# A ring of weight slots moved to multiples of 4 KB in the on-chip memory

## The chip, the core and the metric

The kernel runs on one core of a Trainium2 chip. A core has a matrix engine (TensorE, PE in the profile), a vector engine (VectorE, DVE), a scalar engine (ScalarE, ACT), a general engine (GpSimd, POOL), a sync engine (SyncE, SP) that here issues DMAs, and 16 DMA engines that move data between the chip's HBM and the on-chip memory, the SBUF. The SBUF has 128 partitions; a tile takes the same range of bytes in each of them, and "address" below means the place of that range in a partition. The metric is the device time of one execution in microseconds (us).

## The reference

One decoder layer over 512 tokens of width 1024, all in float32:

```python
h = rmsnorm(x, attn_norm_w[l])
z = h @ w_in[l]
o_a = hgrn2_mixer(...)             # gated linear recurrence, 8 heads
o_b = mla_mixer(...)               # causal attention with low-rank q and kv, 8 heads
y = sigmoid(gate_a) * (o_a @ w_branch_hgrn[l]) + sigmoid(gate_b) * (o_b @ w_branch_mla[l])
x = x + y @ w_out[l]
h = rmsnorm(x, ffn_norm_w[l])
x = x + hierarchical_moe(h, ...)   # 64 experts, each token goes to 2 of one group of 8
return rmsnorm(x, final_norm_w)
```

Every expert is `(silu(xb @ w1) * (xb @ w3)) @ w2`, with w1 and w3 of 1024 x 512 and w2 of 512 x 1024. The three weights of 64 experts are 402.7 MB, and the kernel reads all of them.

## The kernel before, in words

The program has two halves. The first computes the two mixers, the branch products and the output product. Its weights come in pieces of 512 B a row and are split into a high and a low part (L90 and L91), and each product is made of three matrix multiplications (`mm3`). The second half is the experts: 16 blocks of four experts each. A block gathers its tokens by a matrix product (L1069), multiplies by w1 and w3 (`h` in the rows), by w2 (`y`), and adds the rows back to the residual `x2` through another product (`cb` and L1154), for which GpSimd makes a selection matrix out of `slb` (L1088 to L1092).

The experts' weights come as chunks of 8 KB in each partition (1 MB in all). A block has 24 of them. They go through a ring of 22 slots:

```python
RING = ("n",) * 2 + ("y",) + ("x",) * 11 + ("y0",) * 2 + ("wa",) * 2 + ("y2",) * 2 + ("wb",) * 2
```

Each name is a pool of SBUF memory. The slots of `x` (11) lie on the right side of the SBUF, the other 11 on the left side. Where two neighbours are one pool's, they are one tile of 16 KB and one DMA of 2 MB fills both, so that every one of its 128 rows is a single run of 16 KB in HBM and in the SBUF. `prefetch` (L833) issues the DMAs on SyncE's queue in the ring's order. A DMA is issued when the slot's last readers on PE are done. A slot is thus refilled about every 54 us, 27 us for the left slots and 27 us for the right ones. The four w2 parts of the last block come in smaller strips (L845).

Tiles are laid out as they are allocated: pools of the left side grow from address 0 upwards, pools of the right side from the far end downwards, each tile rounded up to 32 B. What stands before the ring on either side sets the addresses of its slots. On the left that is the constants, the small tiles of the pool `keep` (with `rb`, the routers' biases, and `slb`, the slot numbers by block), `small`, and `gl` (with `gT`, the norms' gains). On the right it is `x2` and the experts' working tiles (`xT`, `hid`, `t1`, `owT`, `o1`). In the program as built, every left slot starts 128 B past a multiple of 4096, every right slot 992 B past one; the SBUF is full to its end at 229,344 B.

Of the kernel before, what the change touches and what calls it, by code (L numbers as in the profile page):

```python
# [10 lines left out]
F32 = mybir.dt.float32  # L11
# [9 lines left out]
T = S // 128  # L21
# [11 lines left out]
NB = NE // 4  # L33
# [43 lines left out]
class Trunk:  # L77
# [48 lines left out]
    def run(self):  # L126
        tc, nc, a = self.tc, self.nc, self.a
        const = self.ctx.enter_context(tc.tile_pool(name="const", bufs=1, reuse_waits="tile"))
        cst = const.tile([128, 384], F32, name="cst")
        self.cst = cst  # L130
        self.ident, self.ones, self.iota = [cst[:, i * 128:(i + 1) * 128] for i in range(3)]
        self.keep = self.ctx.enter_context(tc.tile_pool(name="keep", bufs=1, reuse_waits="tile"))
        self.sm = self.ctx.enter_context(tc.tile_pool(name="small", bufs=4, reuse_waits="tile"))
        gl = self.ctx.enter_context(tc.tile_pool(name="gl", bufs=1, reuse_waits="tile"))
        self.ring_open()
        with ExitStack() as right, ExitStack() as left:
            self.mixers(gl, right, left)
        self.moe()


    def mixers(self, gl, right, left):
        tc, nc, a, ident = self.tc, self.nc, self.a, self.ident
        w_in = a["w_in"][0]
        rp = lambda name, bufs=1: right.enter_context(tc.tile_pool(name=name, bufs=bufs, side="right",
                                                                                   reuse_waits="tile"))
# [1 line left out]
        hT = [hp.tile([128, KT, S], F32R, name=f"hT{i}") for i in "hl"]  # L147
        sm = self.sm

        self.gT = gT = gl.tile([128, 46], F32, name="gT")  # L150
        self.fgT = gT[:, 30:38]
        self.lb = gl.tile([128, H], F32, name="lb")
        self.oml = gl.tile([128, H], F32, name="oml")
# [18 lines left out]
        left.close()  # L172


        rc = self.keep
        rb = self.rb = rc.tile([128, 72], F32, name="rb")
        nc.scalar.dma_start(out=rb[:, 0:8], in_=a["router_group_b"].to_broadcast([128, 8]))
        nc.scalar.dma_start(out=rb[:, 8:72], in_=a["router_expert_b"].to_broadcast([128, 64]))
        self.h2p = self.ctx.enter_context(tc.tile_pool(name="h2", bufs=4, reuse_waits="tile"))
# [705 lines left out]
    def route_open(self, rps, gps):  # L885
        nc, mp, iota = self.nc, self.keep, self.iota
        self.rps, self.gps = rps, gps
        self.slb = mp.tile([128, T, 2, NB], F32, name="slb")
        self.wts = mp.tile([128, T, 2], F32, name="wts")
        self.e32 = mp.tile([128, T, 2], F32, name="e32")  # L890
        self.pos = mp.tile([128, T, 2], F32, name="pos")
        self.cnt = mp.tile([128, 1], F32, name="cnt")
        self.fss = mp.tile([128, T], F32, name="fss")
        self.ssq = mp.tile([128, T, 8], F32, name="ssq")
        self.ready = None
        self.h2 = []
        hold = lambda name, shape: mp.tile([128] + shape, F32, name=name)
        self.top = hold("top", [2, T, 8])
        self.ef, self.sl = hold("ef", [T, 2]), hold("sl", [T, 2])
        self.iota8 = hold("iota8", [8])  # L900
        self.fgr = hold("fgr", [8])
        nc.scalar.dma_start(out=self.fgr, in_=self.a["ffn_norm_w"][0].rearrange("(p k) -> p k", k=KT))
        nc.vector.tensor_scalar(out=self.iota8, in0=iota[:, 0:8], scalar1=8.0, scalar2=None, op0=OP.mult)
        self.lps = rps.tile([128, T, 72], F32, name="lgps")
        wr = self.wr
        for kt in range(KT):
            nc.vector.tensor_scalar(out=wr[:, kt], in0=wr[:, kt], scalar1=self.fgT[:, kt:kt + 1],
                                    scalar2=None, op0=OP.mult)
# [382 lines left out]
```

## Time and profile before

| | |
|---|---|
| median of 3 runs | 1597.21 us (1596.31 to 1598.02) |
| the profiled execution's own time | 1594.92 us |
| its span, first to last instruction | 1593.1 us |
| busy share of the span: PE, DVE, ACT, POOL | 86%, 37%, 22%, 15% |
| granted TensorE clock, mean | 0.947 |
| moved by DMA | 458.44 MB, mean 288 GB/s |

PE is busy 86% of the span, but that share is a mean over two halves. The page's lines of 40 slices (a slice is 39.8 us) show the halves: up to slice 17 the DMA engines are busy one to three tenths in most slices, from then on nine tenths. The page's list of the chain of work that ended last goes back from the last instruction through whatever released each step. DMA durations in that chain run from the DMA's issue to its landing, so they hold the time that it stood in the queue.

### The profile page before, as it was taken

The numbers are of one execution on the slowest core, as the hardware profiler recorded it, in microseconds if no ns is written. First come the engines' busy times: TensorE is split into PE (matmuls) and PEld (weight loads), VectorE is DVE, ScalarE is ACT, GpSimd is POOL, SyncE is SP. The second block draws the span as 40 slices with busy tenths as digits, with TensorE's granted clock in tenths as the row PEclk, the third lists the DMA queues.
The fourth block names the chain that finished last, engine by engine and source line by source line (L and its number), as shares of the span: only waits on it lengthen the run. The fifth ranks groups of instructions, "written<-read, shape, count | busy, mean of one in ns | idle before, by whom it ended". The sixth has DMA issues, their size and how long they took to land.

```text
span 1593.1 us, 20247 instructions
## 1 busy us (share of the span) xinstructions
PE 1377.5 (86%) x8248; PEld 837.8 (53%) x8248; DVE 589.3 (37%) x1420; ACT 347.5 (22%) x768; POOL 240.5 (15%) x264
## 2 busy tenths in 40 slices
PE   7999999999999999988888689688688788688785
PEld 7887887887788889833233133233233233223222
DVE  6777767686853333621211111111111111111123
ACT  6666423332332323410100000000000000000012
POOL 1022233323000000012122022022022022022012
PEclk9999999999999999998998899898898899899898
DMA  7111222212163339599999999999999999999997
GB/s 245 62 47 55 71 67 67 67 54 66 53 186 106 93 98 358 214 411 427 425 428 426 426 425 428 426 427 427 427 426 427 427 427 426 425 429 426 425 419 242
DMA packets 124226, 458.44 MB, mean 288 GB/s; under 512 B 12000, under 2 KB 91616, under 8 KB 96992
## 3 DMA queue, kind: packets, MB, share of 16 engines
q1 hardware_dynamic: 121184, 456.47, 71.5%
q8 instruction: 67, 1.10, 0.3%
q10 hardware_dynamic: 2944, 0.62, 0.2%
q14 instruction: 31, 0.25, 0.0%
HBM read 454.97 MB, written 2.10 MB: 287 GB/s over the span
## 4 chain that ended last, share of the span: by engine, by line
PE 58%; DMA 28%; DVE 8%; ACT 3%; issue 1%; POOL 0%; ACTq 0%; DVEq 0%
DMA ck<-in_expert_w 28%; PE z L82 14%; PE h L82 9%; PE y L82 9%; PE ga L1069 7%; PE yacc L82 5%; PE wop L82 2%; PE c L82 2%; PE mx L82 2%; PE z L612 1%; PE cb L82 1%; PE sc L82 1%; PE o L82 1%; DVE rs_u L105 1%; PE lv L82 1%
## 5 line engine op out<-in xcount | busy, mean ns | idle before, releaser
L82 PE MATMUL h<-ck,xT 128*32 128x512 f32 x2048 | 311.3, 664 | 130.8 <-DMA ck<-in_expert_w 111.3
L82 PEld LDWEIGHTS h<-ck,xT 128*32 128x32 f32 x2048 | 73.4, 120 | 355.4 <-issue 167.5
L1088 POOL TENSOR_SCALAR t<-cst,slb,wts 128x128 f32<-128x128 f32 x64 | 50.6, 796 | 967.8 <-PE ga L1069 713.2
L1154 DVE TENSOR_TENSOR x<-cb,x 128x512 f32<-128x512 f32 x120 | 82.9, 691 | 289.0 <-PE cb L82 289.0
L82 PE MATMUL y<-ck,hid 128*32 128x512 f32 (+2 forms) x1088 | 168.7, 577 | 10.9 <-ACT hid L1135 10.1
L91 POOL TENSOR_TENSOR wlo<-wraw,whi 128x1024 fp32r<-128x1024 f32 (+3 forms) x52 | 97.8, 1882 | 266.6 <-ACT whi L90 241.0
L82 PE MATMUL z<-hTh,whi 128*128 128x512 f32 x320 | 127.5, 399 | 5.7 <-ACT vh L616 5.3
L1069 PEld LDWEIGHTS ga<-t,wo 128*128 128x128 f32 x1024 | 117.1, 192 | 25.5 <-issue 24.1
L82 PE MATMUL z<-hTh,wlo 128*128 128x512 f32 x320 | 126.7, 396 | 0.0
L82 PE MATMUL z<-hTl,whi 128*128 128x512 f32 x320 | 126.2, 394 | 0.0
L1069 PE MATMUL ga<-t,wo 128*128 128x128 f32 x1024 | 123.2, 278 | 1.2 <-DVE t L1066 1.2
L82 PE MATMUL cb<-xT,owT 128*128 128x512 f32 (+2 forms) x256 | 120.9, 603 | 2.4 <-DVE xT L1170 2.2
L90 ACT CAST whi<-wraw 128x1024 fp32r<-128x1024 f32 (+3 forms) x84 | 77.5, 923 | 170.0 <-PE z L82 94.2
L1130 DVE TENSOR_TENSOR t<-h,t 128x512 f32<-128x512 f32 x16 | 11.1, 692 | 264.6 <-PE h L82 264.6
L82 PEld LDWEIGHTS y<-ck,hid 128*32 128x32 f32 x1088 | 43.0, 110 | 103.9 <-issue 84.4
L82 PEld LDWEIGHTS cb<-xT,owT 128*128 128x128 f32 x256 | 40.3, 188 | 83.5 <-DVE x L1154 46.9
L1135 ACT COPY hid<-ga 128x512 f32<-128x512 f32 x16 | 9.4, 586 | 299.3 <-PE ga L1133 299.3
L1150 ACT COPY xT<-y 128x512 f32<-128x512 f32 x30 | 17.6, 586 | 257.4 <-PE y L82 257.4
L82 PEld LDWEIGHTS z<-hTh,whi 128*128 128x128 f32 x320 | 60.7, 190 | 18.5 <-ACT vh L616 5.9
L1129 DVE TENSOR_TENSOR t<-h,t 128x512 f32<-128x512 f32 x16 | 11.1, 692 | 156.4 <-ACT t L1128 156.4
L82 PEld LDWEIGHTS z<-hTh,wlo 128*128 128x128 f32 x320 | 60.4, 189 | 12.4
L82 PEld LDWEIGHTS z<-hTl,whi 128*128 128x128 f32 x320 | 60.5, 189 | 11.8
(356 smaller groups left out, 2144.2 us busy)
## 6 DMA issues: line engine op xcount, KB each, us to landing
ck<-in_expert_w SPq DMA_DIRECT2D x164, 2048.0 KB, 34.3
ck<-in_expert_w SPq DMA_DIRECT2D x52, 1024.0 KB, 32.9
wraw<-in_w_in SPq DMA_DIRECT2D x48, 512.0 KB, 3.9
wraw<-in_w_branch_mla SPq DMA_DIRECT2D x8, 512.0 KB, 3.7
wraw<-in_w_branch_hgrn SPq DMA_DIRECT2D x8, 512.0 KB, 3.7
wo<-in_w_out SPq DMA_DIRECT2D x8, 512.0 KB, 5.5
xt<-in_x SPq DMA_DIRECT2D x4, 512.0 KB, 6.0
wraw<-in_mla_w_ukv SPq DMA_DIRECT2D x16, 128.0 KB, 2.4
```

What stands on the lines that cost most here:

```text
L82: self.nc.tensor.matmul(ps, lhsT=l, rhs=r, start=start, stop=stop)
L90: self.nc.scalar.copy(out=hi, in_=src)
L91: (eng or self.nc.vector).tensor_sub(out=lo, in0=src, in1=hi)
L105: nc.vector.tensor_mul(out=u, in0=u, in1=v)
L612: nc.tensor.matmul(ps[t // 2][:, t % 2], lhsT=L[l], rhs=R[r], start=(kt == 0 and n == 0 and t % 2 == 0), stop=(kt == KT - 1 and n == 2), s ...
L1069: nc.tensor.matmul(ps[kt // 4][:, kt % 4], lhsT=self.h2[t][:, kt], rhs=oh[:, t], start=(t == 0 and kt % 4 == 0), stop=(t == T - 1), skip_g ...
L1088: nc.gpsimd.tensor_scalar(out=ow[:, t], in0=iota, scalar1=slot(t, 0), scalar2=wts[:, t, 0:1], op0=OP.is_equal, op1=OP.mult)
L1129: nc.vector.tensor_mul(out=sg, in0=rows(h1), in1=sg)
L1130: nc.vector.tensor_mul(out=sg, in0=rows(h3), in1=sg)
L1135: nc.scalar.copy(out=hid, in_=ps)
L1150: nc.scalar.copy(out=ysb[:, hs], in_=y[half])
L1154: nc.vector.tensor_add(out=self.x2[:, t, hs], in0=ps, in1=self.x2[:, t, hs])
```

## The change

Three small tiles (`gT`, `rb`, `slb`) leave the left side and are allocated first on the right side, in a pool of their own (`rim`), so they lie at the far right end. They take 992 B there. All other right tiles lie 992 B lower. On the left side a tile of 864 B, `fill`, that nothing reads or writes, is allocated in front of the ring; with the three tiles gone and the filler added, the left slots lie 128 B lower.

```diff
@@ run
         gl = self.ctx.enter_context(tc.tile_pool(name="gl", bufs=1, reuse_waits="tile"))
+        self.rim = self.ctx.enter_context(tc.tile_pool(name="rim", bufs=1, side="right", reuse_waits="tile"))
+        self.gT = self.rim.tile([128, 46], F32, name="gT")
+        self.rb = self.rim.tile([128, 72], F32, name="rb")
+        self.slb = self.rim.tile([128, T, 2, NB], F32, name="slb")
+        self.fill = gl.tile([128, 216], F32, name="fill")
         self.ring_open()
@@ mixers
-        self.gT = gT = gl.tile([128, 46], F32, name="gT")
+        gT = self.gT
...
-        rc = self.keep
-        rb = self.rb = rc.tile([128, 72], F32, name="rb")
+        rb = self.rb
@@ route_open
-        self.slb = mp.tile([128, T, 2, NB], F32, name="slb")
```

What it does to addresses, in bytes past a multiple of 4096:

| tiles | before | after |
|---|---|---|
| left slots of the ring (11 of 22) | 128 | 0 |
| right slots of the ring (11 of 22) | 992 | 0 |
| working tiles `xT`, `hid`, `owT` | 992 | 0 |
| working tiles `t1`, `o1` | 3040 | 2048 |
| `x2`, and in the first half `hT` and the weight pieces | 4064 | 3072 |
| first half, most left tiles (`xt`, `craw` of the latent stage) | 1280 | 1152 |

No instruction is added, removed or moved: on all five engines the same instructions stand in the same order with the same semaphore waits in both programs, and they read and write the same HBM addresses. The end of the SBUF's use is the same 229,344 B.

## Rows read from the trace of the kernel before

**Rows 1.** The page's 40 slices of the span: busy tenths of PE, the granted clock, busy tenths of the 16 DMA engines, and what they moved.

```profile
PE   7999999999999999988888689688688788688785
...
PEclk9999999999999999998998899898898899899898
DMA  7111222212163339599999999999999999999997
GB/s 245 62 47 55 71 67 67 67 54 66 53 186 106 93 98 358 214 411 427 425 428 426 426 425 428 426 427 427 427 426 427 427 427 426 425 429 426 425 419 242
```

**Rows 2.** The view of waits over the whole span: who waited for whom, us in total, times, longest.

```profile
PE h L82 <- DMA ck<-in_expert_w: 111.3, 37, 6.3
```

**Rows 3.** The chain of work that ended last, in order of time: start, us, what. Its first and last three pieces that wait for the experts' weights.

```profile
761.09 23.16 DMA ck<-in_expert_w
...
1482.66 32.29 DMA ck<-in_expert_w
1514.96 30.43 DMA ck<-in_expert_w
1545.41 20.95 DMA ck<-in_expert_w
```

**Rows 4.** The page's DMA issues: transfer, queue, count, KB each, median us from issue to landing.

```profile
ck<-in_expert_w SPq DMA_DIRECT2D x164, 2048.0 KB, 34.3
ck<-in_expert_w SPq DMA_DIRECT2D x52, 1024.0 KB, 32.9
```

**Rows 5.** The view by stretches: stretch, us, busy time (and count) of each engine, granted clock, DMA share, GB/s. Three stretches of the experts' half.

```profile
690.00:760.00 70.00, 60.38 (x408) 27.48 (x409) 13.45 (x32) 5.38 (x11) 12.88 (x20) 0.90 1.01 427
760.00:1490.00 730.00, 586.51 (x3456) 221.23 (x3451) 126.85 (x277) 53.96 (x116) 99.46 (x149) 0.91 1.01 427
1490.00:1555.00 65.00, 53.43 (x298) 19.40 (x299) 11.70 (x30) 5.18 (x11) 7.23 (x11) 0.91 1.01 421
```

**Rows 6.** The same view, in six consecutive stretches of 20.5 us in which the packets go to left slots (found by counting the bytes moved, 11 MB to each side in turn; the edges are left out).

```profile
880.20:900.70 20.50, 11.64 (x74) 2.85 (x74) 2.26 (x6) 2.44 (x6) 0.00 (x0) 0.84 1.00 424
934.30:954.80 20.50, 16.02 (x86) 4.51 (x84) 7.05 (x13) 2.44 (x6) 0.24 (x1) 1.00 1.00 424
988.40:1008.90 20.50, 18.11 (x90) 5.18 (x86) 6.65 (x12) 2.55 (x7) 2.04 (x3) 1.00 1.01 426
1042.70:1063.20 20.50, 19.16 (x104) 5.96 (x106) 6.66 (x12) 3.01 (x7) 8.03 (x12) 1.00 1.00 426
1096.80:1117.30 20.50, 20.48 (x112) 9.03 (x110) 4.39 (x7) 1.17 (x2) 8.03 (x12) 1.00 1.00 426
1150.90:1171.40 20.50, 20.44 (x133) 10.93 (x134) 2.26 (x8) 1.18 (x3) 8.03 (x12) 1.00 1.00 424
```

**Rows 7.** The same, in the six stretches of 22.5 us between and beside those, in which the packets go to right slots.

```profile
851.90:874.40 22.50, 21.11 (x137) 11.33 (x138) 3.51 (x11) 1.76 (x3) 8.03 (x12) 1.00 1.01 426
906.10:928.60 22.50, 21.04 (x154) 10.85 (x150) 2.61 (x9) 0.59 (x1) 2.56 (x4) 0.96 1.01 426
960.30:982.80 22.50, 20.79 (x142) 10.58 (x135) 2.62 (x9) 0.59 (x1) 0.61 (x1) 0.95 1.01 428
1014.50:1037.00 22.50, 15.57 (x102) 6.29 (x101) 2.61 (x9) 0.59 (x1) 0.00 (x0) 0.79 1.01 427
1068.60:1091.10 22.50, 12.40 (x65) 2.92 (x64) 1.28 (x2) 0.00 (x0) 0.00 (x0) 0.70 1.01 426
1122.80:1145.30 22.50, 13.14 (x86) 2.93 (x82) 0.69 (x1) 0.60 (x1) 0.00 (x0) 0.77 1.01 430
```

**Rows 8.** The page's DMA issues again: the residual's rows, loaded twice from the same HBM tensor, to `xt` (1280 B past a multiple of 4096) and to `x2` (4064 B past one).

```profile
xt<-in_x SPq DMA_DIRECT2D x4, 512.0 KB, 6.0
...
x<-in_x SPq DMA_DIRECT2D x4, 512.0 KB, 5.9
```

**Rows 9.** Groups of instructions of VectorE by shape: the low part of a weight, 128 x 1024, once with right tiles (`wlo`) and once with left tiles (`wol`); busy us, mean ns of one, idle before.

```profile
L91 DVE TENSOR_TENSOR wlo<-wraw,whi 128x1024 fp32r<-128x1024 f32 x32 | 39.1, 1223 | 49.1 <-ACT whi L90 48.4
...
L91 DVE TENSOR_TENSOR wol<-wo,woh 128x1024 fp32r<-128x1024 f32 x8 | 9.7, 1224 | 6.7 <-ACT woh L90 6.7
```

**Rows 10.** The instructions that read or write the ring's tiles on PE: count, ns min/median/max, first and last start.

```profile
L82 PE MATMUL h<-ck,xT x2048: 589/592/1064, 673.4 to 1560.1; 128*32 128x512 f32 x187
...
L82 PE MATMUL y<-ck,hid x1088: 272/592/1062, 693.3 to 1579.7; 128*32 128x512 f32 x166, 128*32 128x128 f32 x11, 128*32 128x256 f32 x5
```

**Rows 11.** The instructions that read `slb`, the moved tile with the most readers, in the same form, and GpSimd's longest wait.

```profile
L1088 POOL TENSOR_SCALAR t<-cst,slb,wts x64: 792/796/807, 675.7 to 1520.8; 128x128 f32<-128x128 f32 x64
L1090 POOL TENSOR_SCALAR o<-cst,slb,wts x64: 790/792/807, 676.5 to 1523.6; 128x128 f32<-128x128 f32 x64
L1065 DVE TENSOR_SCALAR t<-cst,slb x60: 277/281/288, 692.7 to 1506.4; 128x128 f32<-128x128 f32 x60
...
POOL t L1088 <- PE ga L1069: 713.2, 15, 52.5
```

**Rows 12.** The view by stretches, a short one just after the queue has been refilled.

```profile
684.00:692.00 8.00, 3.91 (x37) 1.21 (x29) 1.38 (x2) 2.47 (x3) 0.89 (x2) 1.00 1.02 434
```

## The prediction

> **What bounds the kernel now.** I read the 40 slices first, then the waits, the chain, and the stretches. In the slices [rows 1] the reader sees two programs: up to about 680 us PE is full and the DMA engines are mostly idle; from there to about 1510 us the DMA engines are full at 425 to 429 GB/s, slice after slice (and at 419 in the one after), while PE has room (six to eight tenths). The waits agree: in the second half PE stands for the experts' weights, 111.3 us in 37 waits [rows 2]. In the chain, from 761.09 us on, every round has a piece that waits for a weight DMA, and the last three, from 1482.66 us to 1545.41 + 20.95 = 1566.36 us, follow each other with nothing between [rows 3]. These pieces are long because a DMA stands some 34 us in the queue before it has landed [rows 4]: at 427 GB/s that is 14.6 MB, seven transfers of 2 MB. The queue is never empty, so when a slot comes free hardly matters, and neither does anything on PE, DVE, ACT or POOL that ends in time. The length of this half is bytes over rate. The rate is 427 GB/s over 690 to 760 us and over 760 to 1490 us, and 421 in the last stretch [rows 5]: a stream of 865 us in which 1% of rate is 8.65 us.
>
> **The change part by part.** No instruction or wait is added, dropped or moved, so there is nothing to count on the engines' paths. What is left is whether an address makes one of the same instructions or packets slower or faster.
>
> The three moved tiles. `slb` has the most readers: 64 + 64 instructions on POOL at 796 and 792 ns and some 120 on DVE [rows 11]. They read one number in a partition as a scalar, out of another address now; nothing in the rows prices an address there, so 0 us. If each of POOL's were 10 ns longer, POOL would spend 1.3 us more over 850 us, and POOL waits 713.2 us for PE there: hidden. `gT` and `rb` are read a few dozen times, 0 us. The filler is never touched, 0 us.
>
> The engines' other operands. Left tiles now lie 128 B lower, right ones 992 B lower. The trace has the same DVE instruction on either side: 128 x 1024 in 1223 ns on tiles 4064 B past a multiple of 4 KB and in 1224 ns on tiles 128 B past one [rows 9]. PE streams the same shape out of slots at 128 and at 992 B: of 2048 products `h`, about half from either side, the shortest takes 589 ns and the median 592 [rows 10]; two levels would show. So 0 us, in the first half as well, where PE and DVE set the end. Cover there is none: 1 ns on each of its 320 x 3 + products would be 1 us, and I keep 1 us either way for it.
>
> The first half's DMAs. The residual is loaded twice from the same HBM rows, to addresses 1280 and 4064 B past a multiple of 4 KB, and takes 6.0 and 5.9 us to land [rows 8]. Those queues are short and hidden by PE: 0 us.
>
> The ring's packets. This is the only term that could count. The trace contains half of the experiment: the left slots start 128 B, the right ones 992 B past a multiple of 4 KB, and the stream goes from one side to the other every 27 us. Six left stretches run at 424, 424, 426, 426, 426, 424 GB/s, mean 425.0 [rows 6]; the six right stretches at 426, 426, 428, 427, 426, 430, mean 427.2 [rows 7]. A stretch is cut at whole packets, so each is good to some 2 GB/s, and the means differ by no more than that. If all slots went like the left ones, the rate would fall from 426.1 to 425.0, 0.26%, +2.2 us; if like the right ones, −2.2 us. The slot that is nearer to an even address (128 is a multiple of 128 B, 992 only of 32 B) is not the faster one. So I take 0 us. What the trace does not show is a packet that starts on a multiple of 4 KB; all 22 slots miss it. For that the price is bounded by the rates that occur. The highest is 434 GB/s, in a short stretch [rows 12]: 865 x (1 − 427/434) = 14.0 us less. The highest of a whole slice in the stream is 429 [rows 1]: 865 x (1 − 427/429) = 4.0 us less. The lowest is 424 [rows 6]: 865 x (427/424 − 1) = 6.1 us more. The value 0 is the one nearest to the rows of both sides; the ends stay for the range. [...]
>
> The sum: 0 us on 1594.92 us, the profiled execution's own time (span 1593.1 us and 1.8 us around it). The median of the runs, 1597.21 us, is 2.3 us above that execution, and the forecast is told on the median: 1597 us, with 1594.5 to 1599.5 as its own range (2.2 us for the sides). A measurement can tell 0.2%, 3.2 us, from no change; that takes a rate that changes by 0.37%, to 428.6 or to 425.4 GB/s.
>
> **The rivals.**
>
> *Each crossing of a 4 KB line costs the DMA engine something.* A row of 16 KB that starts 128 or 992 B past a line touches five such pages, an aligned one four. For it: both sides of the ring pay the same, so the equal rates of rows 6 and 7 do not speak against it, and the stream is purely bound by the packets' time. Against it: the stream has little left to win, and nothing in the rows shows a cost. Priced by the best whole slice, 429 GB/s, it gives −4.0 us, 1593.2 us.
>
> *A row that starts off a smaller boundary makes the engine carry the bytes in front of it.* Then the cost goes with the distance to that boundary, and the two sides must differ, since they start at different distances. The rows have them within 0.5% of each other, with the side that is farther off ahead, 427.2 against 425.0; they leave at most the 14.0 us of the highest rate, which would be 1583.2 us; I take the middle of that and of 4.0 us, −9 us, 1588.2 us. [...]
>
> *Slower: reads and writes fall in step.* After the change every slot and the working tiles `xT`, `hid` and `owT` start at the same place modulo 4 KB, where before a read from a left slot and a write to a right one were 864 B apart. If the memory serves such a pair worse, PE's reads of a slot would hold up the DMA's writes to the next. It would be seen in the experts' half alone, as a lower rate while PE reads. At 424 GB/s, the lowest stretch, it costs 6.1 us: 1603.3 us; it decides from 425.4 GB/s down. For it: the rate does vary by 1%. Against it: the rate does not follow PE. With PE busy 20.48 of 20.5 us it is 426, with 11.64 of 20.5 us it is 424 [rows 6].
>
> *The change does not do what it says* is excluded by the addresses: all slots are multiples of 4096 in the built program.
>
> **How the numbers follow.** No change 0.58 at 1597 us; the crossing 0.22 at 1593.2; the smaller boundary 0.08 at 1588.2; in step 0.12 at 1603.3. The likeliest is the forecast, 1597 us. The range from 1590 to 1601 us holds the first two and the milder part of the third and of the last. Faster by more than 0.2% is 0.22 + 0.08 = 0.30, slower 0.12, no change 0.58.
>
> **What would show it.** In the changed kernel's profile the stretch 760 to 1490 us should again read 427 GB/s and the first expert wait in the chain should again stand near 761 us; then every step is right. If the rate reads 429 or more and all of the gain lies between 690 and 1566 us, the first or the second rival holds; a rate under 425.4 with the same start is the third. If the chain's 761.09 us moves by more than 1 us, an address counts for the engines in the first half, which I took as nothing.

## The result and the profile after

The changed kernel takes 1587.74 us (median of 6 runs, 1587.33 to 1589.03), the kernel before in the same comparison 1596.76 us (6 runs, 1595.42 to 1598.02): a ratio of 0.9946 with a 95% interval of 0.9936 to 0.9957, 9.0 us less by the medians. The profiled executions lie closer together, 1589.03 us against 1594.92 us (spans 1587.2 and 1593.1 us): that of after was the slowest of its six runs, that of before lies below all of its six. The forecast was 1597 us, no change. One execution of e1 below, 2241.23 us at a granted clock of 0.647, was slow and is left out of its time and ratio.

The 40 slices of the changed kernel, to be laid beside [rows 1]: busy tenths of the DMA engines and GB/s.

```profile
DMA  7111222222163338599999999999999999999997
GB/s 246 57 52 54 69 65 73 56 64 67 41 197 95 93 94 330 219 405 429 430 431 429 429 432 430 429 431 430 430 429 430 432 431 429 430 430 431 428 424 253
```

The reader sees the same two halves, and in the second one 428 to 432 GB/s slice after slice where there were 425 to 429 (the last slices, which end the stream, aside). The view by stretches has the same, against [rows 5] (stretch, us, busy time and count by engine, clock, DMA share, GB/s):

```profile
690.00:760.00 70.00, 58.26 (x398) 27.20 (x400) 13.44 (x32) 7.36 (x13) 11.51 (x17) 0.90 1.01 430
760.00:1490.00 730.00, 590.78 (x3471) 222.82 (x3462) 126.86 (x277) 53.95 (x116) 101.01 (x152) 0.91 1.01 430
1490.00:1555.00 65.00, 56.31 (x336) 20.87 (x339) 11.71 (x30) 5.17 (x11) 7.25 (x11) 0.94 1.01 422
```

PE still waits for the experts' weights, 107.8 us against 111.3 us [rows 2]; the kernel is bound by the same thing, which is a little faster:

```profile
PE h L82 <- DMA ck<-in_expert_w: 107.8, 38, 6.2
```

The chain that ended last (start, us, what) keeps its form up to the end. There the last piece that waits for a weight ends at 1545.31 us, where it ended at 1566.36 us before [rows 3], and PE makes the tail. That form of the tail is not the address's doing: in e9 below, whose slots lie as those of the changed kernel do, the last such piece ends at 1559.03 us.

```profile
675.74 13.87 PE h L82 x128
...
762.58 22.83 DMA ck<-in_expert_w
...
1499.42 32.50 DMA ck<-in_expert_w
...
1531.93 13.38 DMA ck<-in_expert_w
```

From the first `h` of the experts to the end it is 1593.1 − 673.44 = 919.7 us before (the chain of before has that `h` at 673.44 us, the first start in [rows 10]) and 1587.2 − 675.74 = 911.5 us after, 8.2 us less. The engines' own work has not changed: VectorE's 128 x 1024 instruction takes 1222 ns on either side, as in [rows 9].

```profile
L91 DVE TENSOR_TENSOR wlo<-wraw,whi 128x1024 fp32r<-128x1024 f32 x32 | 39.1, 1222 | 49.1 <-ACT whi L90 48.4
...
L91 DVE TENSOR_TENSOR wol<-wo,woh 128x1024 fp32r<-128x1024 f32 x8 | 9.7, 1222 | 6.8 <-ACT woh L90 6.7
```

**Where it went, packet by packet.** The trace also holds each DMA packet's start, duration and size, but not its engine. In the stream a packet is one row, of 16 KB or 8 KB. Packets of one engine follow each other without a gap (the next starts 3 or 4 ns before the recorded end of the last, in the kernel before and in the changed one), so they can be chained, and the time from one start to the next is what a row costs. One engine's rows in turn, recorded durations in ns; brackets are the small packet that ends a DMA (size:duration):

```
before  616 611 611 612 [4:9] 619 611 611 622 613 614 615 622 [4:9] 611 611 620 613 614        (left slots)
before  619 613 614 614 621 614 614 614 [4:9] 619 613 614 621 614 614 614 621            (right slots)
after   611 611 611 611 [4:9] 611 611 611 611 611 611 611 611 [4:9] 611 611 611 611 611
```

Means of the start-to-start time between some 750 and 1460 us of the span, intervals lengthened by a packet of another queue left out: before, 610.6 ns for 16 KB rows to left slots and 612.1 ns to right ones; after, 607.1 ns for both. That is 611.4 to 607.1, 0.70%, which over the 865 us of the stream is 6.1 us. The strips of the last block have rows of 2 KB, 1 KB and 512 B, for each engine 128, 128 and 256 of them. Their recorded durations go from 86.8, 48.3 and 29.3 ns to 84.0, 46.0 and 27.0 ns (rows lengthened by half or more left out), about 1.2 us. Some 0.9 us of the 8.2 us is not accounted for by the rows' times.

### The profile page after: what moved, and what is told of

It is laid out like the page before. It is cut to its first block, busy times and chain, and to the rows that moved or that the text cites. A ratio compares the mean times of both kernels' runs of the same rounds, so it can differ in the third digit from the quotient of the medians.

```text
span 1587.2 us, 20247 instructions
## 1 busy us (share of the span) xinstructions
PE 1379.2 (87%) x8248; PEld 841.1 (53%) x8248; DVE 589.4 (37%) x1420; ACT 347.5 (22%) x768; POOL 240.8 (15%) x264
## 4 chain that ended last, share of the span: by engine, by line
PE 59%; DMA 27%; DVE 8%; ACT 3%; issue 1%; POOL 0%; ACTq 0%; SPq 0%; DVEq 0%
DMA ck<-in_expert_w 27%; PE z L82 14%; PE h L82 10%; PE y L82 9%; PE ga L1074 7%; PE yacc L82 5%; PE wop L82 3%; PE c L82 2%; PE mx L82 2%; PE z L618 1%; PE sc L82 1%; PE o L82 1%; DVE rs_u L105 1%; PE lv L82 1%; PE cb L82 1%
## 5 line engine op out<-in xcount | busy, mean ns | idle before, releaser
L82 PE MATMUL h<-ck,xT 128*32 128x512 f32 x2048 | 311.1, 660 | 123.3 <-DMA ck<-in_expert_w 107.8
```

The lines of the kernel that those rows point to most:

```text
L82: self.nc.tensor.matmul(ps, lhsT=l, rhs=r, start=start, stop=stop)
```

## The experiments

What has to be told apart: is it each row's own address, or that all slots (or the engines' tiles) moved together? Which boundary is it: the 4 KB lines that a row crosses, or the place where it starts? Is the price by bytes or by row? Does the source's place in HBM count? The table has all runs; each is read below. "Left" and "right" are the slots' start in bytes past a multiple of 4096, the ns are start to start of 16 KB rows, GB/s is that of 760 to 1490 us in the view by stretches, and the ratio is to the kernel before with its 95% interval.

```
kernel               left  right   left ns  right ns  GB/s   ratio
before                128    992    610.6    612.1    427    1
after                   0      0    607.1    607.1    430    0.9946 [0.9936, 0.9957]
e1 left aligned         0    800    607.4    609.9    429    0.9968 [0.9957, 0.9980]
e2 right aligned     3968      0    607.5    607.1    430    0.9962 [0.9949, 0.9975]
e3 at 512             512    512    607.1    607.1    430    0.9950 [0.9937, 0.9962]
e4 at 256             256    256    607.1    607.1    430    0.9950 [0.9937, 0.9963]
e5 at 128             128    128    611.0    611.0    427    0.9993 [0.9984, 1.0003]
e6 at 224             224    224    612.2    612.2    426    1.0008 [0.9999, 1.0018]
e7 at 32               32     32    612.2    612.2    426    1.0006 [0.9997, 1.0016]
e8 at 64               64     64    611.1    611.1    427    0.9991 [0.9982, 1.0001]
e9 source shifted       0      0    607.1    607.1    430    0.9942 [0.9926, 0.9959]
e10 both shifted      128    992    610.6    612.1    427    0.9999 [0.9990, 1.0009]
e11 rows of 8 KB        0      0    (305.9 for 8 KB)  427    1.0002 [0.9993, 1.0012]
e12 rows of 8 KB      128    992    (310.2 for 8 KB)  420    1.0088 [1.0071, 1.0105]
```

### One side alone

e1 leaves `rb` and `slb` on the left, with a smaller filler:

```diff
         self.gT = self.rim.tile([128, 46], F32, name="gT")
-        self.rb = self.rim.tile([128, 72], F32, name="rb")
-        self.slb = self.rim.tile([128, T, 2, NB], F32, name="slb")
-        self.fill = gl.tile([128, 216], F32, name="fill")
+        self.rb = gl.tile([128, 72], F32, name="rb")
+        self.slb = gl.tile([128, T, 2, NB], F32, name="slb")
+        self.fill = gl.tile([128, 16], F32, name="fill")
```

> Left slots at 0, right slots at 800 bytes past a multiple of 4096 (an odd multiple of 32, as the 992 of before). In the packet records the time from one 16 KB packet's start to the next on its DMA engine was 610.6 ns for left and 612.1 ns for right slots in the kernel before, and 607.1 ns for both in the changed kernel. Theory A (each packet's own address decides): left packets 607.1, right ones about 612; the left side's share of the gain is 3.5 of 8.5 ns, so about 3.7 us of the 9.0 us: 0.9977 of before. Rival B (only all slots together, or the engines' tiles that moved along, bring the gain): left packets stay near 610 and the time is that of before, 0.999 to 1.001.

e2 is the changed kernel with a filler that is 128 B shorter:

```diff
-        self.fill = gl.tile([128, 216], F32, name="fill")
+        self.fill = gl.tile([128, 184], F32, name="fill")
```

> Right slots at 0, left slots at 3968 (128 bytes short of a multiple of 4096). Theory A: right packets 607.1 ns apart, left ones about 610.6; 5.0 of 8.5 ns, so about 5.3 us less: 0.9967 of before. Rival B: both stay at 610 to 612 and the time is that of before.

e1 took 1590.9 us and e2 1588.76 us, the kernel before beside them 1595.66 us: 4.8 and 6.9 us less by the medians. The aligned side's rows go at 607 ns in both, so the rival falls: it is the row's own address. In e1 that holds although the working tiles, which lie on the right, are off a multiple of 256 B there. The stretch from 760 to 1490 us of e1 and of e2:

```profile
760.00:1490.00 730.00, 593.08 (x3478) 225.07 (x3470) 126.84 (x277) 53.95 (x116) 101.82 (x153) 0.91 1.01 429
```

```profile
760.00:1490.00 730.00, 587.94 (x3462) 223.67 (x3464) 126.83 (x277) 53.74 (x116) 98.89 (x149) 0.91 1.01 430
```

But the two gains add up to more than that of both together. By the medians it is 11.7 against 9.0 us, which the intervals alone would allow. From the first `h` to the end, which leaves the scatter of the first half out, e1 takes 1590.5 − 675.78 = 914.7 us and e2 1586.7 − 672.99 = 913.7 us: 5.0 and 6.0 us less than the 919.7 us of before, where both sides together bring 8.2 us. And the side left crooked (off a multiple of 256 B) is also faster than it was: 609.9 instead of 612, and 607.5 instead of 610.6. The rows by their place in the 27 us of a side show why. Mean start to start by DMA, in order, in e1; the first DMA of the right side and the last of the left one have rows of 8 KB, the others of 16 KB:

```
right slots (crooked)   305.9  607.2  607.5  610.9  612.1  611.9
left slots (aligned)    608.5  607.1  607.1  607.1  607.1  305.9
```

After an aligned stretch the crooked rows run at full speed for three DMAs, 24 rows of each engine (305.9 ns is also the time of an aligned row of 8 KB, see e11), then drop to the 612 ns that they have in the kernel before. So the price is put off: for some 24 rows the difference of 5 ns does not show. That is 120 ns, at 16,384 B in 607 ns the time of some 3.2 KB for each engine, an estimate from these numbers. Where aligned stretches come in between, the delay is there anew: the times are means over the stretches of the stream. What puts the price off is not shown, only the delay.

### Which boundary

e3 and e4 put all slots at odd multiples of 512 and of 256 B. e3, against the changed kernel, has `slb` on the left instead of at the right end (480 B are left there) and the same filler; e4 has `gT` and `rb` on the left, 224 B of padding at the right end and a filler of 640 B.

```diff
-        self.slb = self.rim.tile([128, T, 2, NB], F32, name="slb")
+        self.slb = gl.tile([128, T, 2, NB], F32, name="slb")
```

> All slots 512 bytes past a multiple of 4096, so that every 16 KB row still crosses four 4 KB lines inside it. Theory C (the crossings of 4 KB lines cost): packets 610 to 612 ns apart and the time of before, 0.999 to 1.001. Rival D (only a start off a boundary of at most 512 bytes costs): 607.1 ns and the time of the changed kernel, 0.9946.

> All slots 256 bytes past a multiple of 4096. Theory C: as before, 0.999 to 1.001. Rival D with a boundary of 256 bytes or less: 607.1 ns apart and 0.9946 of before; with a boundary of 512 bytes: between 607 and 612.

e3 took 1587.39 us and e4 1588.09 us against 1595.66 us, the time of the changed kernel. In both, rows of 16 KB cross four 4 KB lines, and every one is 607.1 ns after the last. Theory C, the 4 KB lines, falls: a multiple of 256 B is enough. The stretch of e3 and of e4:

```profile
760.00:1490.00 730.00, 588.62 (x3474) 224.27 (x3466) 126.84 (x277) 53.95 (x116) 100.22 (x151) 0.91 1.01 430
```

```profile
760.00:1490.00 730.00, 589.65 (x3483) 224.40 (x3476) 126.84 (x277) 53.95 (x116) 102.35 (x153) 0.91 1.01 430
```

### By bytes, or by row

e5 to e8 put all slots at 128, 224, 32 and 64 B past a multiple of 4096, by moving the three tiles between the sides and by fillers, as in e7:

```diff
-        self.gT = self.rim.tile([128, 46], F32, name="gT")
+        self.gT = gl.tile([128, 46], F32, name="gT")
         self.rb = self.rim.tile([128, 72], F32, name="rb")
         self.slb = self.rim.tile([128, T, 2, NB], F32, name="slb")
-        self.fill = gl.tile([128, 216], F32, name="fill")
+        self.edge = self.rim.tile([128, 40], F32, name="edge")
+        self.fill = gl.tile([128, 176], F32, name="fill")
```

> All slots 128 bytes past a multiple of 4096. Theory E (a row that starts off a multiple of 256 bytes costs the write side a fixed few ns, by how odd its start is): 16 KB packets 610.6 ns apart on both sides, as on the left of the kernel before, and 0.999 of before (2.1 us of the whole time for each ns, from 9.0 us for 4.3 ns). Rival F (the cost grows with the bytes between the 256 byte line and the start; the 128 of the left and the 224 of the right in before): also about 610. The two part at the other offsets.

> All slots 224 bytes past a multiple of 4096 (as far past a 256 byte line as the right slots of before). Theory E and rival F alike: 612.1 ns, 1.001 of before.

> All slots 32 bytes past a multiple of 4096. Theory E: as at 224, about 612 ns apart, 1.001 of before (in e1 the right slots at 800, which is 32 past a 256 byte line, came to 612 late in each stretch). Rival F: a seventh of the cost at 224, so that the read side at 607.1 hides it: 607.1 ns and 0.9946.

> All slots 64 bytes past a multiple of 4096. Theory E: a cost between those at 128 and at 32, 610.6 to 612 ns, 0.999 to 1.001 of before. Rival F: two sevenths of the cost at 224, hidden under the read side: 607.1 ns and 0.9946. Rival G (64 byte lines are what counts): 607.1 ns too, but with 612 in e7.

They took 1594.99, 1597.30, 1596.95 and 1595.23 us, the kernel before beside them 1596.00 us. 32 B past a 256 B line costs as much as 224 B past it (both 612.2 ns, 5.1 over the floor), and 64 B as much as 128 B (611.1 and 611.0, 4 over the floor). So the cost does not go with the bytes between the line and the start, and rivals F and G fall. At the offsets tried it is near enough a fixed 4 to 5 ns for a row that starts off a multiple of 256 B, about 1 ns more where it starts off a multiple of 64 B too. The two offsets of the kernel before stand on the two steps of this stair. Why a start off the line costs this, and why in these two steps, is not shown. e7's stretch reads 426 GB/s:

```profile
760.00:1490.00 730.00, 588.34 (x3464) 223.48 (x3459) 126.93 (x277) 53.86 (x116) 99.99 (x151) 0.91 1.01 426
```

These four kernels also show that new places for the engines' tiles alone bring nothing: in each of them the working tiles, `x2` and the first half's tiles lie elsewhere too, and none is faster than before by more than its interval. In all of these runs the working tiles keep step with the right slots; that a multiple of 256 B is worth nothing to the engines themselves rests on their durations, which did not change (VectorE's 1222 ns against 1223 and 1224, and 795 against 796 ns for GpSimd's `t`, [rows 9, 11]).

### The source's place

e9 (on the changed kernel) and e10 (on the kernel before) read each expert's rows from a place in HBM that is off by 128 B (32 numbers) for left and 992 B (248 numbers) for right slots. The last expert and the strips are left as they were:

```diff
+            self.off = 32 if self.RING[self.nchunk % len(self.RING)] != "x" else 248
...
-        return self.rows(name, e0 + g)[:, half * 2048:(half + n) * 2048]
...
+        by = self.off if e0 + g < NE - 1 else 0
+        flat = self.a[name][0].rearrange("e d f -> (e d f)")[(e0 + g) * 524288 + by:(e0 + g + 1) * 524288 + by]
+        return flat.rearrange("(p c) -> p c", p=128)[:, half * 2048:(half + n) * 2048]
```

> The changed kernel, slots at multiples of 4096, but each expert row (of 63 of the 64 experts) is read from HBM 128 bytes (left slots) or 992 bytes (right slots) past the place where it starts, so the values are those of the wrong columns; sizes, counts and order are the same. Theory H (the place in the SBUF alone decides): 16 KB packets 607.1 ns apart, 0.9946 of before. Rival I (what counts is the shift between the source's and the destination's start): about 611.4 ns and 1.000 of before. Rival J (the read side has a cost of its own for a start off 256 bytes): over 607.1, at least as slow as before if it is of the write side's size.

> The kernel before, slots at 128 and 992 bytes past a multiple of 4096, and each expert row (of 63 of 64) read from HBM 128 or 992 bytes past its start, so that source and destination are off by the same; the values are those of the wrong columns. Theory H: 610.6 and 612.1 ns as before, 1.000 of before, or slower if the read side pays too. Rival I: 607.1 ns, 0.9946 of before.

e9 took 1586.86 us and e10 1595.87 us, beside 1595.83 us before. Shifting the source changes nothing, either with aligned slots (607.1 ns, 430 GB/s) or with crooked ones (610.6 and 612.1 ns, 427 GB/s). Of the two places, that in the SBUF alone decides; rivals I and J fall. e9's stretch:

```profile
760.00:1490.00 730.00, 589.57 (x3474) 225.53 (x3473) 126.90 (x277) 53.86 (x116) 100.11 (x151) 0.91 1.01 430
```

### Twice as many rows

e11 and e12 are the changed kernel and the kernel before with each chunk its own DMA, so that all rows are 8 KB:

```diff
-                pair = (self.paired(self.nchunk) and self.nchunk % 2 == 0
-                        and self.order[self.nchunk + 1] == (b, i + 1))
+                pair = False
```

> The changed kernel with every chunk its own DMA of 1 MB, so that all rows are 8 KB instead of mostly 16 KB; slots at multiples of 4096. Theory K (each row costs a fixed time beside its bytes, on the read side about 4.7 ns: 2 x 305.9 - 607.1; a crooked start adds another 4 to 5 ns on the write side, per row and not per byte): 8 KB packets 305.9 ns apart, 611.8 for 16 KB, 1.000 of before (2.1 us for each ns of 16 KB over 607.1 and 1587.7 us). Rival L (the cost goes with the bytes): 303.6 ns apart and 0.995.

> The same, all rows 8 KB, with the addresses of before (128 and 992). Theory K: 8 KB packets about 310.5 ns apart, 621 for 16 KB, some 29 us over the changed kernel: 1.012 of before, and 1.3 times the difference of e11 to it is due to the start alone, twice the 9 us that it costs with rows of 16 KB. Rival L: 306 ns apart, the time of before, 1.000.

e11 took 1596.45 us and e12 1609.93 us, beside 1596.02 us before. Aligned rows of 8 KB come 305.9 ns apart, 611.8 ns for 16 KB: halving the rows costs an aligned kernel as much as crooked slots cost it with long rows. Crooked rows come 310.2 ns apart, 4.3 ns more, and with 16 KB it was 611.4 − 607.1 = 4.3 ns as well: the price is by row. Rival L falls. (The halved rows also come in 164 more DMAs. In the packet records the 4 B packet at a DMA's end puts off the next row by some 6 ns, about 1 us in all; the row times leave it out.) The same price does not hold for much shorter rows: those of the strips, of 2 KB and less, lost 2.3 to 2.8 ns. That the 607.1 ns, and the 4.7 ns of each row in them, are the reading side's, as the expectations of e7, e8 and e11 have it, was the author's estimate, and no run shows which side sets them. In time, the start alone costs 13.5 us with the short rows (e12 less e11); the expectation of twice 9 us and of 1.012 was too high, since it carried 9.0 us for 4.3 ns over as 2.1 us for each ns, and here it was 13.5 us for 8.6 ns, 1.57 for each. The stretch of e11 and of e12:

```profile
760.00:1490.00 730.00, 586.65 (x3449) 222.44 (x3447) 126.97 (x277) 52.69 (x114) 96.85 (x145) 0.91 1.01 427
```

```profile
760.00:1490.00 730.00, 583.65 (x3414) 223.39 (x3416) 126.28 (x276) 52.68 (x114) 98.05 (x147) 0.90 1.01 420
```

No version beat the changed kernel clearly: e3, e4 and e9 equal it.

## Why the prediction was wrong

**What held.** The stream of weights is the bound, and its length is bytes over rate: the rate rose from 427 to 430 GB/s, 0.7%, and the experts' half became 8.2 us shorter, where 1% was taken as 8.65 us. The moved tiles, the filler and the engines' operands cost nothing that shows, by the durations beside e5 to e8.

**The step that failed** is the one on the ring's packets: "The slot that is nearer to an even address ... is not the faster one. So I take 0 us." In its place the runs show 9.0 us by the medians (8.2 us in the experts' half of the traces): 3.5 ns on every left row and 5.0 ns on every right one. The prediction read the two sides of the ring as an experiment on alignment, one arm at 128 and one at 992 B. By e3 to e8 both arms are on the same side of the boundary: 128 and 992 are both off a multiple of 256 B, and both pay. Equal rates said that the two sides pay alike, not that they pay nothing. The prediction said this itself of the 4 KB lines, and did not carry it over to any smaller boundary.

**The reading was too coarse as well.** The stretches of [rows 6, 7] are good to 2 GB/s, 0.5%, and the whole effect is 0.7%. They even had the sides the wrong way round: by the packets, the right side is the slower one, 612.1 ns against 610.6. The view counts a packet's bytes at its start. Spread over the packets' own durations, the same twelve stretches move 427.1 GB/s on the left and 426.3 on the right in the mean, so the 2.2 GB/s between 427.2 and 425.0 that spoke against the second rival come from the counting. The packets' own times, in the same trace, show both the two sides' steps and rows of 611 ns that neither holds for long.

**The bound held a clue.** The 434 GB/s of [rows 12] was taken as a far end only. As a rate it comes from the counting too: over the packets' own durations the stretch moves 429 GB/s, and the same view gives the changed kernel 439 GB/s from 688 to 696 us, where the stream as a whole runs at 430. So the 14.0 us bounded nothing. The clue is in the packets: the stretch stands just after a pause (the view has 293 GB/s and a DMA share of 0.77 from 676 to 684 us), and every row in it, left or right, has the durations of the changed kernel, 611 ns for 16 KB and 309 ns for 8 KB; within 4 us of its end the rows go to 614 and 621 ns. That is the delay that e1 showed after its aligned stretches.

**The rivals.** The crossing of 4 KB lines (0.22, 1593.2 us) is wrong by e3 and e4. Starting off a smaller boundary (0.08, 1588.2 us) had the right place, the start of the row. Its mechanism, the bytes in front, is wrong, and what it was turned down for, "the cost goes with the distance", is false: 32 B cost what 224 B cost, 612.2 ns a row (e7, e6). That its time was 0.5 us from the result is luck, since it is the middle of 4.0 us and the 14.0 us of the counting. e4 against e5 has the boundary: a row that starts at 256 B takes the 607.1 ns of the changed kernel, one at 128 B 611.0. The source's start, shifted in e9, costs no time (607.1 ns, 430 GB/s). Falling in step (0.12, 1603.3 us) did not happen: all slots at one offset, 0, 256 or 512 B, run at the best rate of all, 430 GB/s.

**The signs named beforehand.** The rate of 430 GB/s and a gain that lies after 690 us are those of the first or second rival. The chain's first expert wait moved from 761.09 to 762.58 us, which the prediction would have laid to addresses in the first half. That is scatter between executions. The first `h` starts at 673.44 us before and 675.74 us after, but e9 and e10, whose tiles all lie as those of after and before, have it the other way round. e9's chain, and e10's:

```profile
673.86 13.87 PE h L82 x128
```

```profile
675.93 13.87 PE h L82 x128
```

## What to carry to other kernels

Where a stream of DMAs into the SBUF is the bound, let each row's destination start at a multiple of 256 B (here 607.1 ns for 16 KB at 256 and 512 B as at 4 KB, e3 and e4) and make the rows long: here a row of 8 or 16 KB costs 4.7 ns beside its bytes, an estimate from 2 x 305.9 − 607.1 (e11 and the changed kernel), and a crooked start another 4 to 5 ns, 0.7% of the row's time with 16 KB and 1.4% with 8 KB. A small tile allocated in front of a ring can move all of its slots off the boundary, so look at the addresses of the built program. And before two halves of a trace are used as an experiment, ask on which side of every possible threshold both of them lie. A rate that counts whole packets in a stretch of 8 or 20 us cannot tell 0.5%; the packets' own times can.

## What was not expected

The cost of a crooked start is hidden for a while: after a pause (the kernel before) or after an aligned stretch of 27 us (e1), some two dozen rows of each engine run at full speed (607 ns for 16 KB) before the stream slows, in e1 to 612. And aligning one half of the ring brought 5.0 or 6.0 of the 8.2 us (e1, e2). The price has two steps, about 4 ns at 64 and 128 B and 5 ns at 32 and 224 B past a 256 B line (e5 to e8). The source's start in HBM, off by 128 or 992 B, cost nothing (e9, 607.1 ns and 430 GB/s; e10, 610.6 and 612.1 ns).
